# Splitting the second latent head group by token halves, and moving half of the output projection between its second halves

## The chip, the cores and the metric

The kernel runs on one core of one Trainium2 chip. The metric is the time of one execution in microseconds on the device. The core has five engines that work side by side, each through its own queue in order: TensorE (PE in the profile; its weight loads are PEld), VectorE (DVE), ScalarE (ACT), GpSimd (POOL) and SyncE (SP), which issues all DMA transfers of this kernel. "x512" and the like are the elements per partition of an instruction; there are 128 partitions.

## What is computed

One layer of a streaming encoder: 1024 tokens of width 1024, two groups of attention heads side by side, one output projection, then a gated MLP with a causal convolution of width 3. Cut to what matters here:

```python
q = rmsnorm(q_lat @ w_q_up);  k, v = split(rmsnorm(kv_lat) @ w_kv_up)      # latent attention, 8 heads
o_mla = softmax(mask(q @ k.T * 96 ** -0.5)) @ v                            # chunk-causal, 1024 x 1024
o_ca  = chunk_attention(cq, ck, cv, rel_bias)                              # 8 heads, band of 9 chunks
mixed = concat([o_mla, o_ca]) @ w_out
x = x + g_a * mixed                                                        # gated residual
h = rmsnorm(x) * (1 + sc_m) + sh_m                                         # "modulated values"
u = causal_dwconv(h @ w_up);  gate, val = split(u)
x = x + g_m * ((silu(gate) * val) @ w_down)
```

The mask lets token block i (128 tokens) see blocks 0 to i, so the first 512 tokens need only the keys of the first 512.

## The kernel before, in words

Matrix products with float32 accuracy are made of three matmuls each: every operand is split into a high part (a rounded copy, `hi_of`, line 71 or 75) and a low part (the rest, `lo_of`, line 82), and high x high, high x low and low x high are summed in PSUM (`gemm3`, lines 150 to 152). A pair of such parts for 512 columns is called a page.

A scheduler orders the instructions of each engine when the program is built. It goes by the order in which the kernel writes them, by priorities (`tc.high_priority` around scores and values), and by which buffers a pool has. Tiles with the same tag share the buffers of that tag; the next tile waits until the oldest buffer is free.

Attention runs through units: a unit is one head and one half of the tokens (`g` 0 or 1, four query blocks each). First come 16 units of the band heads, then the latent heads in two groups of four (`gr` 0 and 1), each head's first half followed by its second half (the list `units`). Per query block, `scores` makes the scores on TensorE, takes the maximum on VectorE, the exponential on ScalarE, scales to a high half on POOL (line 71, `hl`, three buffers) and a low half on VectorE (line 700), and has SP transpose both by DMA (line 702, `PT`, three buffers; blocks wider than 640 in two pieces). `values`, three blocks later, multiplies by the value rows on TensorE (line 713); after four blocks the two parts of the output are joined (lines 720 and 721) and stored to `oT_d` (line 722). A second half has seven pieces to transpose, a first half four.

Between these steps `pace` lets a list of fillers issue their matmuls, in proportion to the unit's own cost (`R_CA` 1.9, `R_MLA` 0.5): the projections of the inputs, and last `f_oca`, which multiplies the band heads' output by its half of `w_out` and stores the partial sums to `part_d`. Side work (`f_ada`) makes the modulation rows.

After attention, for each of eight token tiles t (from line 868): the latent output `ol` is loaded and split, multiplied by the other half of `w_out` (`op`, 24 matmuls), added to the loaded partial `pa` (line 884), multiplied by the gate row `gabc` (885), added to the residual `x1` (886), stored (887), squared and summed (888), and scaled by the inverse root mean square (891). After tile 3, eight pages of modulated values of the first 512 tokens are transposed and scaled (`mod_T`, lines 855 to 857, two PSUM buffers); they give the pages `b11` and `b21`.

The MLP's up projection is a scheme of seven block products over token halves (as in Strassen's method). It needs the pages b11, b21 (first half), b22 (second half) and t1 to t4 (sums and differences). After tile 7 a loop over k = 0 to 3 makes, for each k, the transposes of the second half and then one page each of t3, t1, b22, t2, t4 (lines 942 to 952). Then `ff_tile` runs for 22 tiles of the hidden width; tile 0's first product needs t3 and the split of the weight difference `ws3` ("ws", line 1012; "wc", its split). The down projection ends the kernel.

## Time and profile before

| | us |
|---|---|
| three timed runs, median (lowest, highest) | 1463.82 (1462.19, 1465.44) |
| profiled execution, span from first to last instruction | 1461.0 |
| PE busy in it | 1273.7 (87%) |
| DVE busy | 1028.2 (70%) |
| POOL busy | 780.0 (53%) |
| ACT busy | 611.7 (42%) |

Of the profiled execution its span is what is shown. A page of the profile gives busy times, the span in 40 slices, the groups of instructions by line, and the DMA issues. The trace behind it can be asked for busy times in chosen stretches, for the instructions in order of time, and for what ended an engine's idle time. A row of the timeline has the start, the length, the engine, the line, the operation, what it writes and reads, how many are merged, and in brackets the idle time before it with its releaser. A row of groups has the count after "x", then busy time, the mean length of one in ns, and the idle time before. Line numbers are those of the kernel before, where nothing else is said.

### The profile page before, as it was taken

Reading aid. Unit: us, or ns where it says so; the run is one execution under the profiler, and the core shown is the slowest. Engines: PE = TensorE matmul, PEld = TensorE weight load, DVE = VectorE, ACT = ScalarE, POOL = GpSimd, SP = SyncE. Lnnn points to the kernel's source line nnn. Section 1 sums busy time; section 2 is a strip of 40 time slices with the busy share of each in tenths; the row PEclk is TensorE's granted clock in tenths of the full one; section 3 lists DMA queues with packets and bytes.
Section 4 is the critical chain, followed back from the end, with each engine's and each line's share of the span. In section 5 each row is a group of like instructions: output and inputs, shape, how many; then the busy total and the mean of one; then the engine's idle time right before and its main releaser. Section 6 shows DMA issues by size and latency. Waiting matters only on the chain.

```text
span 1461.0 us, 20153 instructions
## 1 busy us (share of the span) xinstructions
PE 1273.7 (87%) x6836; PEld 1053.1 (72%) x6836; DVE 1028.2 (70%) x1830; ACT 611.7 (42%) x1190; POOL 780.0 (53%) x717
## 2 busy tenths in 40 slices
PE   3859989998867788885776999999999998999997
PEld 2749878886746666764555888788888887887885
DVE  6874776476798968772487887777777777566653
ACT  4544354343455545443273434334444433332331
POOL 5263554274555745444545555566555555665662
PEclk9979987999788899996887999999999999999998
DMA  7323547455522577869611323322222234446442
GB/s 282 134 71 75 131 113 150 126 122 116 115 64 45 127 153 161 175 139 270 223 72 63 111 100 108 109 87 87 87 87 87 77 137 162 151 144 237 148 142 101
DMA packets 218595, 185.94 MB, mean 127 GB/s; under 512 B 148086, under 2 KB 183034, under 8 KB 217468
## 3 DMA queue, kind: packets, MB, share of 16 engines
q1 hardware_dynamic: 218492, 184.66, 44.0%
q8 instruction: 54, 0.88, 0.2%
q14 instruction: 49, 0.40, 0.1%
HBM read 121.17 MB, written 28.84 MB: 103 GB/s over the span
## 4 chain that ended last, share of the span: by engine, by line
PE 39%; DMA 18%; DVE 16%; POOL 12%; issue 11%; ACT 3%; SPq 1%; DVEq 0%; POOLq 0%; ACTq 0%
POOL wds L82 5%; PE p L921 4%; PE p L923 4%; PE p L922 4%; DMA aw<-w_ada 4%; DMA PTm<-hlm 3%; DMA wu<-w_up 3%; PE sc L655 3%; PE dnp L1064 2%; PE dnp L1066 2%; PE dnp L1065 2%; PE sm L655 2%; DMA PTc<-hlc 2%; DVE adacc L243 2%; DMA cl<-oT_d 1%
## 5 line engine op out<-in xcount | busy, mean ns | idle before, releaser
L82 POOL TENSOR_TENSOR wds<-wd,wds 128x512 fp32r<-128x512 f32 x88 | 153.6, 1766 | 100.7 <-ACT wds L75 100.7
L82 POOL TENSOR_TENSOR wc<-ws,wc 128x512 fp32r<-128x512 f32 x22 | 65.4, 2975 | 134.7 <-ACT wc L75 134.7
L1054 DVE TENSOR_TENSOR wd<-wd,gmbc 128x1024 f32<-128x1024 f32 x44 | 69.4, 1577 | 80.7 <-DMA wd<-w_down 78.1
L1064 PE MATMUL dnp<-wds,g 128*128 128x512 f32 x308 | 119.9, 391 | 2.8 <-DVE xo L1072 2.3
L1066 PE MATMUL dnp<-wds,g 128*128 128x512 f32 x308 | 118.5, 390 | 3.8 <-DVE g L82 3.8
L75 ACT ACTIVATE wds<-wd 128x512 fp32r<-128x512 f32 x88 | 54.8, 624 | 157.8 <-PE dnp L1066 152.7
L1065 PE MATMUL dnp<-wds,g 128*128 128x512 f32 x308 | 119.6, 389 | 0.0
L71 POOL TENSOR_SCALAR hlm<-Pm,rim 128x512 f16<-128x512 f32 (+4 forms) x88 | 66.5, 760 | 58.1 <-DMA PTm<-hlm 37.0
L71 POOL TENSOR_SCALAR hlc<-Pc,ric 128x640 f16<-128x640 f32 (+2 forms) x64 | 45.6, 715 | 79.2 <-DVE ric L683 40.1
L700 DVE SCALAR_TENSOR_TENSOR hlm<-Pm,rim,hlm 128x512 f16<-128x512 f32 (+4 forms) x88 | 66.1, 758 | 23.3 <-POOL hlm L71 23.0
L1012 DVE TENSOR_TENSOR ws<-wu,wu 128x512 f32<-128x512 f32 x22 | 28.1, 1279 | 75.6 <-DMA wu<-w_up 75.6
L655 PE MATMUL sm<-mk,mq 96*128 96x512 f32 (+3 forms) x288 | 71.1, 378 | 10.3 <-ACT Pm L680 9.3
L82 DVE TENSOR_TENSOR g<-gr,g 128x512 fp32r<-128x512 f32 x44 | 71.0, 1616 | 11.4 <-ACT g L75 11.4
L998 DVE SCALAR_TENSOR_TENSOR u<-c,pk,u 128x1023 f32<-128x1023 f32 x44 | 77.4, 1765 | 1.8 <-ACT u L997 1.8
L1033 ACT ACTIVATE u<-u 128x1024 f32<-128x1024 f32 x22 | 23.4, 1063 | 132.0 <-DVE u L999 132.0
L713 PE MATMUL pvm<-PTm,vt 128*128 128x128 f16 x576 | 49.4, 239 | 33.5 <-DMA PTm<-hlm 28.6
L680 ACT ACTIVATE Pc<-sc,mc 128x640 f32<-128x640 f32 (+2 forms) x64 | 42.2, 659 | 86.2 <-DVE mc L670 61.7
L997 ACT ACTIVATE u<-c,pk 128x1024 f32<-128x1024 f32 x44 | 52.3, 1236 | 55.2 <-DVE c L1029 55.2
L430 DVE SCALAR_TENSOR_TENSOR aacc<-aw,cs,aacc 128x256 f32<-128x256 f32 x84 | 44.7, 532 | 43.5 <-DMA aw<-w_ada 42.9
L655 PE MATMUL sc<-k,q 64*128 64x512 f32 (+3 forms) x288 | 70.1, 372 | 5.3 <-ACT Pc L680 3.0
L713 PEld LDWEIGHTS <-vt 128*128 128x128 f16 x576 | 40.6, 108 | 46.3 <-issue 41.2
L1066 PEld LDWEIGHTS dnp<-wds,g 128*128 128x128 f32 x308 | 57.8, 188 | 17.1 <-DVE g L82 5.0
(366 smaller groups left out, 4308.0 us busy)
## 6 DMA issues: line engine op xcount, KB each, us to landing
wu<-w_up SPq DMA_DIRECT2D x44, 512.0 KB, 3.9
wd<-w_down SPq DMA_DIRECT2D x44, 512.0 KB, 4.4
aw<-w_ada SPq DMA_DIRECT2D x96, 128.0 KB, 2.3
g_d<-u SPq DMA_DIRECT2D x22, 512.0 KB, 2.6
gr<-g_d SPq DMA_DIRECT2D x44, 256.0 KB, 3.6
x<-x SPq DMA_DIRECT2D x16, 512.0 KB, 8.0
adaw<-w_ada_a SPq DMA_DIRECT2D x8, 1024.0 KB, 5.6
wq_r<-w_qk SPq DMA_DIRECT2D x32, 128.0 KB, 2.5
```

The lines of the kernel that those rows point to most:

```text
L71: pool.tensor_scalar(o, i, s, 1.0, op0=MUL, op1=MUL)
L82: (pool if eng == "p" else dve).tensor_tensor(o, i, f32(hi), op=SUB)
L655: last = pe.matmul(s[:, c:c + w], qpg[rs_, a, q], kpgs[kh][rs_, b, ko:ko + w], start=(a == 0 and b == 0), stop=(a == 1))
L700: dve.scalar_tensor_tensor(hl[:, w:2 * w], pp, ri[:], hl[:, :w], op0=MUL, op1=SUB)
L713: last = pe.matmul(u.pv[:, c], u.vst(j), mov, start=(x == 0), stop=(x == len(todo) - 1))
L921: pe.matmul(pt, sh, pg[:, 0], start=(k == 0), stop=False)
L922: pe.matmul(pt, sh, pg[:, 1], start=False, stop=False)
L998: dve.scalar_tensor_tensor(u[:, 1:], c[:, :S - 1], pk[:, cv + 1:cv + 2], u[:, 1:], op0=MUL, op1=ADD)
L1054: dve.tensor_tensor(raw[:], raw[:], gmbc[:], op=MUL)
L1064: pe.matmul(pts[t][n], sh, w[n][:, 0], start=(j == 0), stop=False)
L1065: pe.matmul(pts[t][n], sh, w[n][:, 1], start=False, stop=False)
L1066: pe.matmul(pts[t][n], sl, w[n][:, 0], start=False, stop=(j == NF - 1))
```

## The change

The second group's units are put in another order: first the first halves of its four heads, then the four second halves, beginning with head 3. So that keys of the first halves are still there for the second halves, those of three heads are kept in buffers of the tag `v16`, which held values of the band heads. `R_MLA` goes from 0.5 to 0.95, so `f_oca` ends with the first halves. A new filler, `f_first`, then issues what stood behind attention for tokens 0 to 511: the loads of `ol`, `x`, the gate row and the partials, the projection in column halves, residual, norm, and the eight transposed and scaled pages `v0`. These pages use the one PSUM buffer of tag "T". They are copied by DMA to another pool (`v0c`), where the rest of the kernel reads them. The loop behind attention keeps tiles 4 to 7. The pages of the second half are written kind by kind: all transposes, then t3 for the four k, then t2, t1, t4 and b22. The two parts of a unit's output are joined in the output's own buffer.

```diff
-R_CA, R_MLA = 1.9, 0.5
+R_CA, R_MLA = 1.9, 0.95
...
+    def f_first():
+        wo.extend(load_wo(0, n, "a", "p") for n in range(2))
+        ga = []
+        for n in range(2):
+            ga.append(G["v"].tile([P, 512], F32, name=f"gah{n}", tag="Gv", bufs=8))
+            sp.dma_start(ga[n][:], ga_d[:, n * 512:(n + 1) * 512])
+        xs = []
+        for t in range(4):
+            lo = rtile(f"ol{t}", (P, 4, P), F32R)
+            hi = rtile(f"oh{t}", (P, 4, P), F32R)
+            sp.dma_start(f32(lo[:]), oT_d[0:4, :, t * P:(t + 1) * P].rearrange("k p t -> p k t"))
+            hi_of("a", hi[:], f32(lo[:]))
+            lo_of("p", lo[:], f32(lo[:]), hi[:])
+            x1 = pgtile([P, D], F32, f"x1_{t}")
+            sp.dma_start(x1[:], I["x"][t * P:(t + 1) * P, :])
+            for n in range(2):
+                c = slice(n * 512, (n + 1) * 512)
+                pa = qtile(f"pa{t}_{n}")
+                sp.dma_start(pa[:], part_d[t][:, c])
+                pt = ps.tile([P, 512], F32, name=f"op{t}_{n}", tag="mm", bufs=2)
+                yield from gemm3_f(pt[:], [(hi[:, k], lo[:, k], wo[n][k][:, 0], wo[n][k][:, 1]) for k in range(4)])
+                dve.tensor_tensor(pa[:], pa[:], pt[:], op=ADD)
+                pool.tensor_tensor(pa[:], pa[:], ga[n][:], op=MUL)
+                pool.tensor_tensor(x1[:, c], x1[:, c], pa[:], op=ADD)
+                act.activation(pa[:], x1[:, c], AF.Square, accum_out=ss2[:, t, n:n + 1])
+            sp.dma_start(x1_d[t], x1[:])
+            pool.tensor_tensor(ss2[:, t, 0:1], ss2[:, t, 0:1], ss2[:, t, 1:2], op=ADD)
+            rsqrt_mean(r2[:, t:t + 1], ss2[:, t, 0:1], D)
+            act.activation(x1[:], x1[:], AF.Copy, scale=r2[:, t:t + 1])
+            xs.append(x1)
+        for k in range(ND):
+            pt = ps.tile([P, 512], F32, name=f"ht_ps2_{k}_0", tag="T", bufs=TB)
+            for j in range(4):
+                pe.transpose(pt[:, j * P:(j + 1) * P], xs[j][:, k * P:(k + 1) * P], ident[:])
+            v0[k] = g3([P, 512], F32, f"v0_{k}")
+            act.activation(v0[k][:], pt[:], AF.Identity, scale=modT[:, 2, k:k + 1], bias=modT[:, 3, k:k + 1])
+            yield 436
...
+        if tag == "v16":
+            hi, lo = [apg.tile([P, 512], F32R, name=f"{name}_{i}", tag="v16", bufs=6)[:] for i in "hl"]
...
-                    act.activation(sb[r0], u.pv[r1], AF.Copy, scale=inv[r1])
-                    dve.scalar_tensor_tensor(dst[r0], u.pv[r0], inv[r0], sb[r0], op0=MUL, op1=ADD)
+                    act.activation(dst[r0], u.pv[r1], AF.Copy, scale=inv[r1])
+                    dve.scalar_tensor_tensor(dst[r0], u.pv[r0], inv[r0], dst[r0], op0=MUL, op1=ADD)
...
+            kept = gr == 1 and g == 0 and hh < 3
...
-               ("m", f_m()), ("up0", f_up(0)), ("up1", f_up(1)), ("oca", f_oca())]
+               ("m", f_m()), ("up0", f_up(0)), ("up1", f_up(1)), ("oca", f_oca()), ("first", f_first())]
+    half_done = [False]
...
+            if key == "first" and not half_done[0]:
+                return None
...
-    units += [mla_unit(gr, hh, g) for gr in range(2) for hh in range(4) for g in range(2)]
+    units += [mla_unit(0, hh, g) for hh in range(4) for g in range(2)]
+    units += [mla_unit(1, hh, 0) for hh in range(4)]
+    first_half = 4 * len(units)
+    units += [mla_unit(1, hh, 1) for hh in (3, 0, 1, 2)]
...
-            pace(u.values(i), R_CA if u.band else R_MLA)
-    need(["oca"])
-    for _ in side[0]:
-        pass
-    wo = [load_wo(0, n, "a", "v" if n else "p") for n in range(2)]
+            cost = u.values(i)
+            if n - DEPTH + 1 == first_half:
+                need(["oca"])
+                for _ in side[0]:
+                    pass
+                half_done[0] = True
+            pace(cost, R_CA if u.band else R_MLA)
+    need(["first"])
...
+    for k in range(ND):
+        v = vtile(f"v0c_{k}")
+        sp.dma_start(v[:], v0[k][:])
+        v0[k] = v
...
-    for t in range(NT):
+    for t in range(4, NT):
...
-        lo_of("p", lo[:], f32(lo[:]), hi[:])
-        x1 = tb.tile([P, D], F32, name=f"x1_{t}", tag="x1", bufs=8)
+        lo_of("v" if t % 2 else "p", lo[:], f32(lo[:]), hi[:])
+        x1 = tb.tile([P, D], F32, name=f"x1_{t}", tag="x1", bufs=4)
...
-        if t % 4 == 3:
-            h = t // 4
-            if h == 0:
-                for k in range(ND):
-                    v0[k] = mod_T(k, 0)
-                    bpage("b11" if k < 4 else "b21", k % 4, v0[k], "v" if k % 2 else "p")
+    for k in range(ND):
+        bpage("b11" if k < 4 else "b21", k % 4, v0[k], "v" if k % 2 else "p")
...
+    b12 = [mod_T(k) for k in range(4)]
+    b22 = [mod_T(k) for k in range(4, ND)]
     for k in range(4):
-        b12, b22 = mod_T(k, 1), mod_T(k + 4, 1)
-        t3 = tb.tile([P, 512], F32, name=f"t3_{k}", tag="v", bufs=11)
-        dve.tensor_tensor(t3[:], b22[:], b12[:], op=SUB)
+        t3 = vtile(f"t3_{k}")
+        dve.tensor_tensor(t3[:], b22[k][:], b12[k][:], op=SUB)
         bpage("t3", k, t3, "v")
-        dve.tensor_tensor(b12[:], b12[:], v0[k][:], op=SUB)
-        bpage("t1", k, b12, "v")
-        bpage("b22", k, b22, "v")
-        dve.tensor_tensor(b22[:], b22[:], b12[:], op=SUB)
-        bpage("t2", k, b22, "v")
-        dve.tensor_tensor(v0[k + 4][:], v0[k + 4][:], b22[:], op=SUB)
+    for k in range(4):
+        dve.tensor_tensor(b12[k][:], b12[k][:], v0[k][:], op=SUB)
+        t2 = vtile(f"t2_{k}")
+        dve.tensor_tensor(t2[:], b22[k][:], b12[k][:], op=SUB)
+        bpage("t2", k, t2, "v")
+        dve.tensor_tensor(v0[k + 4][:], v0[k + 4][:], t2[:], op=SUB)
+    for k in range(4):
+        bpage("t1", k, b12[k], "v")
+    for k in range(4):
         bpage("t4", k, v0[k + 4], "v")
+    for k in range(4):
+        bpage("b22", k, b22[k], "v")
```

More of the change, by code (lines that the diff above doesn't have):

```diff
@@ L615, in qk_page @@
             pe.transpose(pt[:rows, j * P:(j + 1) * P], src(j), ident[:])
-        pg = at.tile([P, 2, 512], F32R, name=name, tag=tag, bufs=bufs)
+        if tag == "v16":
+            hi, lo = [apg.tile([P, 512], F32R, name=f"{name}_{i}", tag="v16", bufs=6)[:] for i in "hl"]
+        else:
+            pg = at.tile([P, 2, 512], F32R, name=name, tag=tag, bufs=bufs)
+            hi, lo = pg[:, 0], pg[:, 1]
         if gain is None:
-            act.activation(pg[:rows, 0], pt[:rows], AF.Copy)
-            dve.tensor_tensor(pg[:rows, 1], pt[:rows], f32(pg[:rows, 0]), op=SUB)
-        else:
-            act.activation(pg[:rows, 0], pt[:rows], AF.Copy, scale=gain)
-            dve.scalar_tensor_tensor(pg[:rows, 1], pt[:rows], gain, f32(pg[:rows, 0]), op0=MUL, op1=SUB)
-        return pg
+            act.activation(hi[:rows], pt[:rows], AF.Copy)
+            dve.tensor_tensor(lo[:rows], pt[:rows], f32(hi[:rows]), op=SUB)
+        else:
+            act.activation(hi[:rows], pt[:rows], AF.Copy, scale=gain)
+            dve.scalar_tensor_tensor(lo[:rows], pt[:rows], gain, f32(hi[:rows]), op0=MUL, op1=SUB)
+        return hi, lo
     class Unit:
@@ L654, in scores @@
                         for b in range(2 - a):
-                            last = pe.matmul(s[:, c:c + w], qpg[rs_, a, q], kpgs[kh][rs_, b, ko:ko + w],
+                            last = pe.matmul(s[:, c:c + w], qpg[a][rs_, q], kpgs[kh][b][rs_, ko:ko + w],
                                              start=(a == 0 and b == 0), stop=(a == 1))
@@ L765, in mla_unit @@
         u.prep = prep
[L766 removed]
+        u.need = ["up1"] if gr or g else ["up0"]
         u.needv = []
@@ L784, in fill_step @@
                 continue
-            if key not in ("v0", "up0", "up1", "oca"):
+            if key not in ("v0", "up0", "up1", "oca", "first"):
                 nside[0] += c
@@ L864, in bpage @@
         B[nm, k] = pg
-    ss2 = cst.tile([P, NT], F32, name="ss2")
-    r2 = cst.tile([P, NT], F32, name="r2")
     xn2 = {}
```

32 lines of the change are left out of this document (18 added, 14 removed).

## The prediction

> **What bounds it now.** I read the page first, then busy times stage by stage, then the chain of waits from 640 to 800 us, then the order in which the changed program's instructions stand on each queue.
>
> ```profile
> span 1461.0 us, 20153 instructions
> PE   3859989998867788885776999999999998999997
> PEclk9979987999788899996887999999999999999998
> ```
>
> The span is 1461.0 us; the three timed runs have a median of 1463.8, 2.8 more, and I add my difference to that median. TensorE is full from the 22nd slice (767 us on) and has holes before it. The stages, with PE busy time first:
>
> ```profile
> core 0: us, PE busy (x) PEld busy (x) DVE busy (x) ACT busy (x) POOL busy (x), PEclk, DMA share, GB/s
> 500.00:571.60 71.60, 62.61 (x409) 49.24 (x408) 53.51 (x134) 33.63 (x73) 35.65 (x41) 0.92 0.73 158
> 571.60:649.00 77.40, 64.28 (x447) 51.90 (x447) 58.61 (x145) 38.77 (x82) 36.50 (x44) 0.93 0.75 158
> 649.00:676.00 27.00, 15.97 (x123) 13.42 (x120) 13.83 (x30) 8.60 (x19) 10.52 (x13) 0.73 0.82 168
> 676.00:742.70 66.70, 51.26 (x209) 40.30 (x210) 28.44 (x25) 22.06 (x38) 40.09 (x34) 0.83 0.70 249
> 742.70:777.80 35.10, 14.32 (x73) 10.55 (x71) 30.99 (x46) 24.44 (x40) 5.20 (x7) 0.71 0.04 15
> 795.10:1180.00 384.90, 381.22 (x1672) 313.17 (x1671) 302.79 (x277) 160.25 (x225) 227.50 (x140) 1.00 0.26 95
> ```
>
> From 795 us TensorE is busy 381 of 385 us at full clock: 1672 matmuls, 0.230 us each. Nothing after that point is edited, so the change is worth what it moves the first product of the MLP (the "wc" product of tile 0). Before that stand latent attention (to 676), the output projection of eight token tiles (to 742.7), and the pages (to 777.8), where VectorE is busy 31 of 35 us and TensorE 14. The marks I count from:
>
> ```profile
> 669.64 0.69 POOL L71 TENSOR_SCALAR hlm<-Pm,rim 128x512 f16<-128x512 f32 x1 [1.44 <-DMA PTm<-hlm]
> 674.95 1.01 PE L713 MATMUL pvm<-PTm,vt 128*128 128x128 f16 x8 [1.71 <-DMA PTm<-hlm]
> 742.32 0.39 PE L152 MATMUL op<-wo,ol 128*128 128x512 f32 x1
> 751.26 1.13 DVE L891 TENSOR_SCALAR x<-x,r 128x1024 f32<-128x1024 f32 x1 [2.15 <-DMA x_d<-x]
> 754.29 0.69 DVE L944 TENSOR_TENSOR t<-hv,hv 128x512 f32<-128x512 f32 x1 [1.30 <-ACT hv L857]
> 776.38 0.68 DVE L1012 TENSOR_TENSOR ws<-wu,wu 128x512 f32<-128x512 f32 x1
> 777.84 0.80 PE L921 MATMUL p<-t,wc 128*128 128x512 f32 x1 [14.11 <-ACT wc L75]
> ```
>
> The last attention value ends at 675.96 and the MLP begins at 777.84: 101.9 us. The last POOL half of a probability piece starts 6.3 us before that value ends. The 36 VectorE page instructions run from 754.29 to 776.38, and the subtraction that feeds the first product stands behind them all on VectorE.
>
> **Attention, part one of the sum.** The change puts 96 projection matmuls (tokens 0 to 511) among the four second halves; 84 of them stand before the last value, the last 12 behind it. Does attention have room? I cut the stage at the first transpose of each half unit and counted the old filler (tile oc), short halves first, long ones after:
>
> ```profile
> 596.00:606.20 10.20, 0.38 (x2) 0.30 (x2) 0.00 (x0) 0.00 (x0) 0.83 0.59 129
> 544.90:557.60 12.70, 7.04 (x25) 4.01 (x23) 0.00 (x0) 0.60 (x1) 1.00 0.64 115
> 557.60:571.60 14.00, 2.06 (x7) 1.06 (x6) 0.00 (x0) 1.18 (x2) 1.00 0.97 211
> 606.20:621.90 15.70, 9.19 (x36) 6.00 (x34) 0.00 (x0) 1.16 (x2) 1.00 0.94 203
> 523.30:544.90 21.60, 12.13 (x37) 7.68 (x36) 0.00 (x0) 1.79 (x3) 0.84 0.71 158
> ```
>
> 23 more matmuls lengthen a short half by 2.5 us (0.11 each); 29 or 30 more lengthen a long one by 1.7 or 7.6 (0.06 or 0.25). I take 0.10: 84 x 0.10 = 8.4 us. The ends are nothing, if all of it runs in the holes (PE is busy 143 of the 176 us, so 33 are idle), and 84 x 0.230 = 19.3 us, if TensorE pays for each. The other load of the new filler falls on POOL:
>
> ```profile
> L71 POOL TENSOR_SCALAR hlm<-Pm,rim 128x512 f16<-128x512 f32 (+4 forms) x70 | 48.4, 695 | 52.9 <-DMA PTm<-hlm 36.3 <-DVE rim L683 6.3 <-DVE sm L673 3.9
> L82 POOL TENSOR_TENSOR cl<-cl,ch 128x512 fp32r<-128x512 f32 x16 | 21.9, 1368 | 28.6 <-ACT ch L75 26.3 <-PE mq_ps L615 2.2
> ```
>
> In the last long half seven pieces of 0.7 us (4.9) get eight 512-wide operations of about 1.3 us and three short ones (some 1.5) between them: 16.8 us on a queue that has 14 to 16. I add 0.6 us for that, so the last value comes 9 us later (675.96 to 685). Multiplications by the gate row that were VectorE's are POOL's here; each also waits for its load of the stored partial, for which there are two buffers, and the pieces queued behind it wait too. That is the same POOL time, counted once. Weight loads and splits (16 instructions) are those of before, earlier.
>
> **From the last value to the MLP, part two.** Prices:
>
> ```profile
> L857 ACT ACTIVATE hv<-ht_ps,modT 128x512 f32<-128x512 f32 x16 | 11.8, 775 | 7.0 <-PE ht_ps L855 7.0
> L888 ACT ACTIVATE pa<-x 128x1024 f32<-128x1024 f32 x8 | 8.5, 1059 | 16.5 <-POOL x L886 13.7 <-DVE x L886 2.7
> L884 DVE TENSOR_TENSOR pa<-pa,op 128x1024 f32<-128x1024 f32 x8 | 9.7, 1219 | 24.5 <-PE op L152 24.5
> L116 POOL TENSOR_TENSOR r<-ss,nhalf 128x1 f32<-128x1 f32 x8 | 6.4, 799 | 0.5
> 743.00 1.03 PE L855 MATMUL ht_ps<-ident,x 128*128 128x128 f32 x8
> 752.80 1.45 ACT L857 ACTIVATE hv<-ht_ps,modT 128x512 f32<-128x512 f32 x2 [2.08 <-PE ht_ps L855]
> 760.95 1.12 PE L855 MATMUL ht_ps<-ident,x 128*128 128x128 f32 x4 [1.54 <-ACT hv L857]
> 681.65 0.80 PE L150 MATMUL op<-wo,oh 128*128 128x512 f32 x1 [5.69 <-ACT oh L75]
> ```
>
> (a) Token tile 3 has to be finished: 17.3 us. Its second partial can be loaded only when the square of tile 2 has freed a buffer. From the last POOL piece: five 1.3 us operations, three short ones, two waits for the first partial of tile 3 give 13.2 us until that square is done; then, with the gaps, load 3.8 (behind a 512 KB store), add 0.8, multiply and add on POOL 2.6, square 0.8, mean and power 1.2, scale 1.2: 23.6, less the 6.3 us up to the last value. The floor is 10, if the partials wait for nothing. (b) Eight pages of transposes through one PSUM buffer, each followed by its activation: 1.12 + 0.78 + 0.1 = 2.0 us, 16 us in all; warm (the eight transposes in 1.03 us at 743.00) it would be 12. Before, these pages lay under the projection of tiles 4 to 7.
>
> The Trainium skill, page "TensorE: Matmul & The Clock Gate", section "Part 4: PE-mode transpose", says that transposes do not count as the activity that raises the clock. By that the 16 us hold; if transposes did raise it the sum would be 4 us less. The quoted row is cold but had idle time before it, so the trace does not decide it.
>
> (c) In the SP order the eight copies of those pages (line 909 of the changed kernel) stand ahead of the four x loads, the gate row and the first load of the second half's attention output. SP waits in order, so that output is asked for only after the eighth page, behind five transfers of 512 KB:
>
> ```profile
> wu<-w_up SPq DMA_DIRECT2D x44, 512.0 KB, 3.9
> ol<-oT_d SPq DMA_DIRECT2D x8, 256.0 KB, 4.0
> DMA packets 5757, 9.76 MB, mean 349 GB/s; under 512 B 400, under 2 KB 3472, under 8 KB 5755
> ```
>
> The second row is on the page, the third is 676 to 704 us, where the queue was full. A lone output load issued 2.8 us after the page would land at 6.8; 2.9 MB at 349 to 410 GB/s behind 3 us of issue and latency land at 10.2. I take 10.2 and 0.7 for its high part: 10.9 (7.5 to 12). Before, nothing stood ahead of those loads but weights, and the projection began at 681.65. (d) Four token tiles are 96 matmuls, 22.1 us, and 2 us for a cold start as at 681.65: 24.1. The gain of the change is here: before, eight tiles took 742.71 - 681.65 = 61 us with their waits. (e) Tile 7 from its last matmul to its scaled rows took 752.39 - 742.71 = 9.7 us; I take 8.7, since POOL has no page work beside VectorE. (f) Scaled rows to the first product took 25.5 us. **Pages kind by kind** do not shorten it: the same 36 VectorE instructions stand ahead of the "ws" subtraction in the changed order too. They begin later: VectorE's first needs the fifth activation (5.9 us after the scaling by cold transposes and 0.68 us a page), where it needed the second (1.9). I add 3.7: 29.2.
>
> Sum: 17.3 + 16 + 10.9 + 24.1 + 8.7 + 29.2 = 106.2 us against 101.9, 4.3 more.
>
> **The rest** I put at nothing: three kept key heads in old value buffers and half outputs combined in place remove no instruction and wait for stores 10 us old; the product of the first two page kinds with tile 0 (24 matmuls, 5.5 us) lies under (e), and stood there in part before; the lower halves of odd tiles go from POOL to VectorE under running matmuls.
>
> **Sum.** 9 + 4.3 = 13.3 us: the span 1474.3, the time 1463.8 + 13.3 = **1477.1 us**.
>
> **Rivals.** First, faster: attention gets shorter. A short half takes 10.2 us and more for four transposes (2.5 us each), a long one 14 for seven (2.0). If the short ones are slow only because they alternate with long ones, four in a row at 2.0 save 12 us (11 less 8, four times), and the filler runs free in waits. Then the last value comes 12 us earlier, and 4.3 - 12 gives -7.7: 1456.1. It decides at a last value before 671.7. For it speak the idle PE; against it that a short tile has the same chain (maximum, exponential, two halves, transpose) as a long one. Second, the filler is paid in full: TensorE and POOL queues hold each other up, 19.3 + 4.3 = 23.6: 1487.4. Third, the pages do work kind by kind: VectorE's 19th of 36 instructions ends the first kind, so the MLP could begin 17 x 0.61 = 10.4 us earlier: 1466.7; the order of VectorE speaks against it, since "ws" stands last. Fourth, the tail's waits are at their floors (10, 12 and 7.5 in (a) to (c)): 14.7 less, 1462.4.
>
> **Chances.** Forecast 0.53 (own range 1468 to 1484), attention shorter 0.11, paid in full 0.20, kind by kind 0.04, floors 0.12. A measurement of this kernel can tell about 0.2%, 2.9 us. Faster by more: the first rival and a little of the fourth, 0.13; within: most of the fourth and part of the third, 0.12; slower 0.75. The range leaves out most of the first rival and the top of the second: 1460 to 1490.
>
> **What would show it.** The last value (pvm, then om) at about 685 and not before 672; after it TensorE nearly idle for 40 us but for 32 transposes with an activation after each four; copies v0c on SP, then x, then ol; the wc product behind all 36 page instructions, 106 us after the last value; equal times from there on. I am wrong if attention ends early, if ol is issued before the copies end, or if wc runs while pages are still made. Weakest is the price of a filler matmul, 0 to 0.23 us, and the two-buffer chain of (a).

## The result, and the profile after

The changed kernel takes 1482.88 us (median of four runs, 1481.71 to 1487.18) against 1464.57 for the kernel before (four runs, 1462.19 to 1465.44): a ratio of 1.0127, with a 95% interval of 1.0103 to 1.0151. It is slower, as forecast, by 18.3 us where 13.3 were forecast. The profiled execution has a span 20.4 us longer. From its page:

```profile
span 1481.4 us, 20209 instructions
PE   3859989998968788986384999999999999999996
PEclk9879987999789898988596999999999999999999
```

A slice is 37.0 us. Before the long row of nines stand a 3 (704 to 741 us, most of the stretch between the last attention value and the projection of tile 4), an 8 (that projection) and a 4 (the pages of the second half). The stages after, cut at the marks the prediction used (PE busy first):

```profile
572.20:618.80 46.60, 41.77 (x251) 33.75 (x249) 32.90 (x87) 24.93 (x55) 18.64 (x25) 0.93 0.71 180
618.80:691.70 72.90, 57.39 (x369) 43.53 (x368) 47.74 (x85) 28.56 (x57) 48.45 (x51) 0.86 0.84 192
691.70:709.10 17.40, 3.67 (x15) 2.50 (x14) 2.71 (x4) 6.27 (x10) 9.51 (x13) 0.73 0.32 111
709.10:724.40 15.30, 8.28 (x29) 5.19 (x29) 0.00 (x0) 6.28 (x10) 0.00 (x0) 0.50 0.32 120
724.40:735.70 11.30, 0.00 (x0) 0.00 (x0) 6.30 (x4) 4.74 (x9) 6.29 (x4) 0.50 0.90 332
735.70:760.40 24.70, 24.56 (x97) 19.67 (x98) 13.82 (x10) 6.21 (x10) 11.64 (x11) 0.90 0.50 179
760.40:768.80 8.40, 6.21 (x30) 4.84 (x28) 5.05 (x5) 2.34 (x5) 1.48 (x4) 1.00 0.30 121
768.80:797.40 28.60, 5.49 (x26) 3.74 (x26) 23.20 (x40) 17.84 (x29) 0.00 (x0) 0.61 0.00 0
```

The first two rows are the second latent group: the four first halves, then the four second halves. The other six are the steps (a) to (f) of the prediction: 17.4, 15.3, 11.3, 24.7, 8.4 and 28.6 us, 105.7 in all, where it said 17.3, 16, 10.9, 24.1, 8.7 and 29.2, 106.2 in all. The same group before, from the last value of the first group to its own:

```profile
575.00:676.00 101.00, 76.85 (x542) 62.40 (x540) 69.89 (x167) 44.53 (x93) 44.91 (x54) 0.88 0.76 161
```

So the second latent group went from 101.0 to 119.5 us, 18.5 more, on 78 more matmuls and 22 us more of POOL. Of those matmuls 65 are filler: the group holds 75 of the old filler (tile oc) and 84 of the new one, where it held 94 of the old. The whole account of the 20.4 us: the first group ends 2.8 earlier (572.2 instead of 575.0), the second takes 18.5 more, the tail 3.8 more (105.7 against 101.9), tile 0 of the MLP 1.0 less, everything from tile 1 on 1.8 more (20.3, to within rounding). The table gives the same marks for every kernel run; M is the end of the first group, L the last value, O the first projection matmul of tile 4, W the first product of tile 0, N the first matmul of tile 1, all in us and from the timelines. The two stages on both sides of O are left empty where the projection of tiles 0 to 3 lies between L and O.

| kernel | M to L | L to O | O to W | M to W | W to N | N to end | time us |
|---|---|---|---|---|---|---|---|
| before | 101.0 | | | 202.8 | 17.3 | 665.9 | 1464.6 |
| changed | 119.5 | 44.0 | 61.7 | 225.2 | 16.3 | 667.7 | 1482.9 |
| e1 filler let go late | 124.6 | 34.7 | 63.0 | 222.4 | 16.4 | 668.8 | 1481.8 |
| e2 a third of the matmuls | 111.4 | 45.8 | 61.9 | 219.1 | 16.7 | 668.6 | 1481.1 |
| e3 gate on VectorE | 119.7 | 32.4 | 61.7 | 213.9 | 16.8 | 668.3 | 1471.8 |
| e4 four partial buffers | 125.6 | 21.5 | 61.6 | 208.6 | 16.3 | 667.5 | 1469.6 |
| e5 order only (from before) | 100.3 | | | 205.9 | 17.1 | 664.6 | 1471.6 |
| e6 two PSUM buffers | 117.7 | 37.0 | 62.1 | 216.8 | 17.3 | 665.8 | 1475.4 |
| e7 load of tile 4 ahead | 118.3 | 33.7 | 69.5 | 221.5 | 16.9 | 669.3 | 1483.4 |
| e8 weight parts ahead | 116.4 | 44.4 | 43.2 | 204.0 | 27.0 | 673.0 | 1478.5 |
| e9 four repairs | 129.8 | 19.5 | 62.2 | 211.4 | 17.2 | 668.7 | 1479.1 |
| e10 e9 and weight parts | 130.4 | 19.5 | 43.0 | 193.0 | 27.0 | 672.8 | 1473.8 |
| e11 pages only (from before) | 101.8 | | | 189.0 | 30.5 | 668.6 | 1470.1 |
| e12 e9 and loads ahead | 126.5 | 7.8 | 70.7 | 205.0 | 17.1 | 667.2 | 1473.6 |

Times of e1 to e8 are single runs, the others are medians; the ratios given with an interval are worked out over all runs and differ a little from those of the medians. Runs of the kernel before made beside the experiments lie between 1461 and 1474, so a single time is good to about 6 us; stages are read from them instead. Between the changed kernel, e6, e7 and e8, which do not differ up to L, M to L varies from 116.4 to 119.5: about 3 us is the scatter of a stage.

### The profile page after: what moved, and what is told of

Same layout as the page of the kernel before. It is cut to its first block, busy times and chain, and to the rows that moved or that the text cites. A ratio compares the mean times of both kernels' runs of the same rounds, so it can differ in the third digit from the quotient of the medians.

```text
span 1481.4 us, 20209 instructions
## 1 busy us (share of the span) xinstructions
PE 1285.4 (87%) x6836; PEld 1059.8 (72%) x6836; DVE 1030.9 (70%) x1826; ACT 618.6 (42%) x1202; POOL 790.6 (53%) x733
## 4 chain that ended last, share of the span: by engine, by line
PE 53%; DMA 14%; DVE 11%; POOL 9%; issue 8%; ACT 3%; SPq 1%; DVEq 0%; POOLq 0%; ACTq 0%
PE p L980 8%; PE p L982 8%; PE p L981 8%; POOL wds L82 5%; PE sc L701 3%; DMA PTm<-hlm 3%; DMA aw<-w_ada 3%; PE dnp L1129 2%; PE dnp L1130 2%; PE dnp L1131 2%; DVE adacc L243 2%; PE pvc L759 1%; PE sm L701 1%; PE ipv L150 1%; PE ipv L151 1%
## 5 line engine op out<-in xcount | busy, mean ns | idle before, releaser
L1130 PE MATMUL dnp<-wds,g 128*128 128x512 f32 x308 | 119.5, 389 | 0.0
L71 POOL TENSOR_SCALAR hlm<-Pm,rim 128x512 f16<-128x512 f32 (+4 forms) x88 | 65.3, 748 | 44.9 <-DMA PTm<-hlm 30.5
L71 POOL TENSOR_SCALAR hlc<-Pc,ric 128x640 f16<-128x640 f32 (+2 forms) x64 | 45.8, 717 | 74.1 <-DVE ric L729 37.2
L746 DVE SCALAR_TENSOR_TENSOR hlm<-Pm,rim,hlm 128x512 f16<-128x512 f32 (+4 forms) x88 | 70.2, 808 | 21.4 <-POOL hlm L71 21.4
L1131 PEld LDWEIGHTS dnp<-wds,g 128*128 128x128 f32 x308 | 57.8, 188 | 17.1 <-DVE g L82 5.1
L1129 PEld LDWEIGHTS dnp<-wds,g 128*128 128x128 f32 x308 | 57.8, 188 | 15.1 <-DVE xo L1137 2.7
L1130 PEld LDWEIGHTS dnp<-wds,g 128*128 128x128 f32 x308 | 57.8, 188 | 11.8
```

The lines of the kernel that those rows point to most:

```text
L71: pool.tensor_scalar(o, i, s, 1.0, op0=MUL, op1=MUL)
L746: dve.scalar_tensor_tensor(hl[:, w:2 * w], pp, ri[:], hl[:, :w], op0=MUL, op1=SUB)
L1129: pe.matmul(pts[t][n], sh, w[n][:, 0], start=(j == 0), stop=False)
L1130: pe.matmul(pts[t][n], sh, w[n][:, 1], start=False, stop=False)
L1131: pe.matmul(pts[t][n], sl, w[n][:, 0], start=False, stop=(j == NF - 1))
```

## The experiments

The prediction's tail came out term by term; its attention term did not (9 forecast, 15.8 later by the last value, 18.5 by the group's length). Theory A: TensorE pays for each filler matmul (the second rival, 0.19 to 0.23 us each). Theory B: the order of the units costs it. Theory C: the filler's other work, its POOL operations and its two-buffer chain of loads, holds up the queues, which run in order.

### e1_behind: the filler let go after the last value

```diff
-                half_done[0] = True
...
+    half_done[0] = True
     need(["first"])
```

> The changed kernel, but the filler with the first half's projection is let go only after the last attention value, so that the four second halves run with no filler at all; everything else is as changed. This measures the price of the 84 matmuls in attention. In the changed kernel the last value ends at 691.7 us of the span. Theory A (TensorE pays for each matmul, and the order of the units costs nothing): 84 x 0.19 to 0.23 less, the last value at 672 to 676. Theory B (the new order of the units itself is slower): it stays above 684. The whole is then longer than the changed kernel, since the same matmuls with their two-buffer chain stand bare behind attention: 1482.9 - 17 + 8 x 3.5 = about 1494 us.

Missed, and not what the edit was for. The scheduler orders instructions by readiness, not by where they are written: 96 projection matmuls still ran before the last value, nearly all in the last two second halves (2 in that of head 0, 70 in that of head 1, 24 in that of head 2), and the last value came at 697.1. It prices nothing; it shows only that the filler does not run later for being let go later in the program's text. M to W is 2.8 us less than in the changed kernel, within scatter.

### e2_third: two thirds of the filler's matmuls left out

```diff
-                yield from gemm3_f(pt[:], [(hi[:, k], lo[:, k], wo[n][k][:, 0], wo[n][k][:, 1]) for k in range(4)])
+                for k in range(4):
+                    with tc.issue_after(trail[-1 - LAG]):
+                        pe.matmul(pt[:], hi[:, k], wo[n][k][:, 0], start=k == 0, stop=k == 3)
+                    if k % 2:
+                        yield 6 * (512 / 2.4 + 2.5)
```

> The changed kernel with only the high x high matmul of the first half's projection (4 of 12 for each column half; the two correction products are left out, so the result lacks them); all loads, splits, gate products, squares and the pacing stay. Theory A (TensorE time is what the filler costs): 56 of the 84 matmuls in attention fall away at 0.19, so the last value comes 10.6 us earlier, at 681, and the time is about 1471. Theory C (what costs is the chain of load, add, gate product, residual, square, through two buffers and the POOL queue, with TensorE waiting in order): less than 3 us, last value at 689 or later, time 1480.

Between the two. Twenty-four filler matmuls are left before the last value instead of 84, and the group is 8.1 us shorter (119.5 to 111.4): 0.135 us per matmul. But it is still 10 us longer than before with nearly the same number of matmuls. Its four first halves and its four second halves:

```profile
575.00:620.10 45.10, 40.09 (x250) 32.11 (x249) 33.08 (x88) 25.06 (x56) 18.17 (x24) 0.96 0.73 187
620.10:686.40 66.30, 46.28 (x309) 35.42 (x308) 44.59 (x84) 27.13 (x53) 46.43 (x46) 0.77 0.88 202
```

POOL is busy 64.6 us in the group, where it had 44.9 before, so the filler's other work is the first suspect for the 10 us. The next run says where they stand.

### e5_order_only: the new order of the units alone

```diff
-    units += [mla_unit(gr, hh, g) for gr in range(2) for hh in range(4) for g in range(2)]
+    units += [mla_unit(0, hh, g) for hh in range(4) for g in range(2)]
+    units += [mla_unit(1, hh, 0) for hh in range(4)]
+    units += [mla_unit(1, hh, 1) for hh in (3, 0, 1, 2)]
```

(on the kernel before, with the kept keys and the joined halves of the change)

> The kernel before with the new order of the units alone (second latent group: four first halves, then the second halves of heads 3, 0, 1, 2, keys kept, output parts joined in place); the old filler at its old ratio, the whole projection behind attention as before. Theory B (the order itself costs what attention got longer by): last value 685 to 692 us of the span instead of 676. Theory C (the order is free, the new filler's chain costs): 673 to 679 and the time within 3 us of the kernel before. My first rival before the result (first halves in a row are faster): 664.

The group takes 100.3 us (101.0 before): the order is free at the old filler's ratio, and theory B falls. The last value is at 682.5 only because this execution reached the group 7 us later (M at 582.2); the expectation was written in marks of the span, which carry that. The first halves in a row are faster (34.1 us for four, from the ends of their last values, against 42.2 when they alternated), and the second halves slower by nearly as much (66.2 against 58.8), so the first rival of the prediction saw something real that came back within the group. The same two stretches as for e2:

```profile
582.20:616.30 34.10, 30.13 (x191) 24.07 (x192) 27.17 (x77) 20.27 (x46) 16.25 (x22) 0.89 0.72 157
616.30:682.50 66.20, 51.72 (x360) 42.60 (x359) 42.18 (x90) 25.04 (x48) 27.99 (x32) 0.81 0.84 162
```

Beside e2 they move the suspicion. The 11.1 us between the two runs lie in the first halves (45.1 against 34.1), where the new filler has not been let go: none of its POOL operations stands there, and POOL is busy 18.2 and 16.3 us. The second halves, where all of the new filler's POOL work is, take 66.3 and 66.2 us. What fills the first halves is the old filler, which at an `R_MLA` of 0.95 ends there:

| | first halves, us | old filler matmuls in them | second halves, us | filler matmuls in them |
|---|---|---|---|---|
| before | 42.2 | 40 | 58.8 | 54, old |
| e5 order only | 34.1 | 35 | 66.2 | 59, old |
| e2 a third of the matmuls | 45.1 | 75 | 66.3 | 24, new |
| changed | 46.5 | 75 | 72.9 | 84, new |

In a row the first halves leave TensorE little room: it is busy 30.1 of 34.1 us in e5 and 41.7 of 46.5 in the changed kernel. Of these 11.5 us more, 10.95 are the old filler's matmuls (22.87 against 11.92 us busy); the 12 score matmuls that run ahead into the stretch (63 against 51) take 1.8, less what overlaps. So theory A fits the first halves, for matmuls that the prediction left out. In the second halves the 60 matmuls between the changed kernel and e2 are worth 6.6 us. What the new filler's other work costs there can only be estimated: e2 has 35 filler matmuls fewer than e5 and gains nothing, which at 0.135 us each would be 5 us. No run changes `R_MLA` alone; this division is read from the stages of single executions, with their 3 us of scatter.

### e3_gate_dve and e4_pa4: POOL's share, and the buffers

```diff
-                pool.tensor_tensor(pa[:], pa[:], ga[n][:], op=MUL)
-                pool.tensor_tensor(x1[:, c], x1[:, c], pa[:], op=ADD)
+                dve.tensor_tensor(pa[:], pa[:], ga[n][:], op=MUL)
+                dve.tensor_tensor(x1[:, c], x1[:, c], pa[:], op=ADD)
```

> The changed kernel with the gate product and the residual sum of the filler on VectorE instead of POOL. Theory A: no change of the last value (691.7 within 2 us). Theory C, POOL part (probability pieces wait behind 1.3 us operations on POOL): the last value 4 to 8 us earlier, at 684 to 688, and the time 1475 to 1479.

```diff
+        pap = [pgtile([P, D], F32, f"pap{i}") for i in range(2)]
...
-                pa = qtile(f"pa{t}_{n}")
-                sp.dma_start(pa[:], part_d[t][:, c])
+                pa = pap[t % 2][:, c]
+                sp.dma_start(pa, part_d[t][:, c])
```

> The changed kernel with four half-row buffers for the loaded partials instead of two (two idle page buffers taken). Theory A: last value unchanged (691.7 within 2 us). Theory C, buffer part (the load waits for the square of two pieces earlier and stands on the transfer queue behind transposes that wait for POOL): last value 5 to 7 us earlier, and the finish of token tile 3, 17.4 us from the last value to its scaled rows, falls to 10 to 13; the time is then 1470 to 1474.

First the chain as it stands in the changed kernel, from its timeline in the last second half:

```profile
676.83 0.53 SPq L633 DMA_DIRECT2D pa<-part_d  x1
681.05 0.69 DVE L636 TENSOR_TENSOR pa<-pa,op 128x512 f32<-128x512 f32 x1 [2.62 <-DMA pa<-part_d]
681.79 0.79 PE L150 MATMUL op<-wo,oh 128*128 128x512 f32 x1 [4.17 <-DVE pa L636]
681.81 1.72 POOL L637 TENSOR_TENSOR pa<-pa,gah 128x512 f32<-128x512 f32 x1 [2.31 <-DMA ol<-oT_d]
684.09 0.63 PE L152 MATMUL op<-wo,ol 128*128 128x512 f32 x1
684.75 0.69 POOL L71 TENSOR_SCALAR hlm<-Pm,rim 128x512 f16<-128x512 f32 x1
```

The partial is asked for at 676.83, lands four microseconds later, and only then can VectorE add it and free a PSUM buffer. TensorE stood 4.17 us with the next filler matmul at the head of its queue, attention values behind it, and came back on a slow clock (rows of 0.63 us instead of 0.40, a matmul every 0.43 us instead of 0.23). POOL stood 2.31 us at the gate product (its row names a transfer, but the addition that it needs ended at 681.74), and the last probability piece, behind it, was scaled at 684.75. The waits of TensorE on that addition, from the last first half to past tile 3, in the changed kernel and in e3 (engine, waiting line, released by; us in total, times, longest):

```profile
PE op L150 <- DVE pa L636: 6.3, 2, 4.2
```

```profile
PE op L150 <- DVE pa L636: 0.5, 1, 0.5
```

In e4 the line is gone. Both edits miss where they were aimed and gain elsewhere. The group did not get shorter (119.7 and 125.6 us): the filler, no longer held, put all of its 96 matmuls and 3 and 10 of the page transposes ahead of the last value. But tile 3 was ready 5.3 us after the last value in e3, and 6.4 before it in e4, instead of 17.4 after, and O came 11.4 and 16.4 us earlier counted from M. So the chain is a true cost of the change, some 11 to 16 us up to O, and it was spread over attention and step (a).

### e6_ht_mm: two PSUM buffers for the pages

```diff
-            pt = ps.tile([P, 512], F32, name=f"ht_ps2_{k}_0", tag="T", bufs=TB)
+            pt = ps.tile([P, 512], F32, name=f"ht_ps2_{k}_0", tag="mm", bufs=2)
```

> The changed kernel with the eight transposed pages of the first half going through the two PSUM buffers of the projection instead of one. In the changed kernel they take 15.2 us from the scaled rows of tile 3 to the last activation (2.0 a page). If one buffer is the cause, a page then takes the slower of four transposes (0.9 to 1.1 us) and one activation (0.8), 9 to 10 us in all, and the copies, the loads behind them and everything later come 5 to 6 us earlier: 1477. If the transposes themselves are the limit, less than 2 us.

Here the theory holds: the pages take 7.9 us instead of 15.3, and the projection of tile 4 begins 7 us sooner after the last value (37.0 against 44.0). The stage and its transposes:

```profile
708.40:716.30 7.90, 6.36 (x26) 4.65 (x26) 0.00 (x0) 5.98 (x9) 0.00 (x0) 0.58 0.54 197
```

```profile
709.75 5.70 PE L648 MATMUL ht_ps<-ident,x 128*128 128x128 f32 x24 [0.66 <-ACT v L650]
```

In the changed kernel each page's transposes took 1.12 of 2.0 us, and the granted clock was 0.50 over the whole 15.3 us. Here twenty-four transposes follow each other for 5.7 us without a hole, and the clock rises at the end of them:

```profile
711.70:715.00 3.30, 3.27 (x15) 2.58 (x15) 0.00 (x0) 2.46 (x4) 0.00 (x0) 0.50 0.71 262
715.10:718.40 3.30, 0.35 (x3) 0.11 (x1) 0.95 (x1) 3.30 (x7) 1.48 (x2) 1.00 0.84 292
```

The Trainium skill's sentence on transposes (page "TensorE: Matmul & The Clock Gate", section "Part 4: PE-mode transpose"), that they do not count as the activity that raises the clock, does not hold here: from 708.40 to 715.1 TensorE ran nothing but transposes, and the granted clock went from 0.50 to 1.00. The second half's pages show the same (in e9 0.50 from 758.60 to 761.90, with 15 transposes and nothing else on TensorE, and 1.00 from 762.10). The measurement decides. Step (b)'s 16 us came out all the same: with one buffer TensorE was busy 8.28 of the 15.3 us, and the clock stayed at 0.50.

### e7_ol4_ahead: the transfer queue

```diff
+    o4 = [tb.tile([P, 4, P], F32R, name=f"o{i}4", tag=f"o{i}4", bufs=1) for i in "lh"]
+    sp.dma_start(f32(o4[0][:]), oT_d[0:4, :, 512:640].rearrange("k p t -> p k t"))
+    hi_of("a", o4[1][:], f32(o4[0][:]))
+    lo_of("p", o4[0][:], f32(o4[0][:]), o4[1][:])
     for k in range(ND):
         v = vtile(f"v0c_{k}")
```

> The changed kernel with the attention output of tile 4 loaded and split from buffers of its own, its load ahead of the eight page copies on the transfer queue. If the queue order is what costs 11.3 us between the last page and the first projection matmul of tile 4, that falls to 1 to 2 us and the time by 8 to 10, to 1473 to 1475; if the later loads (tile 5, the x rows, the partials) are as late as before and hold the projection, less than 4 us of it remain.

The queue before the edit:

```profile
710.49 14.36 SPq L909 DMA_DIRECT2D v0c<-v  x8
724.90 2.03 SPq L940 DMA_DIRECT2D x<-x  x4
726.97 0.54 SPq L932 DMA_DIRECT2D gabc<-ga_d  x1
727.56 0.47 SPq L936 DMA_DIRECT2D ol<-oT_d  x1
735.02 0.63 ACT L75 ACTIVATE oh<-ol 128x512 fp32r<-128x512 f32 x1 [6.51 <-DMA ol<-oT_d]
```

SP issues in order and waits for each page; the load that TensorE needs is issued at 727.56, lands before 735.02. With the load ahead of the copies tile 4 began 0.6 us after the last page, 10 us sooner, as expected. But only the wait moved: tile 5's own load was then late, and TensorE waited for it 4.76 us,

```profile
738.39 0.79 PE L150 MATMUL op<-wo,oh 128*128 128x512 f32 x1 [4.76 <-ACT oh L75]
```

so O to W grew from 61.7 to 69.5, and of the 10 us between L and O 2.4 remain at W; the single time, 1483.4, shows no gain. The second reading of the expectation was the right one.

### e8_ws_tb and e11_before_ws: kind by kind

```diff
+    ws3 = mt("w2", [P, 2, 512], "ws3_0")[:, 0]
+    wc0 = tb.tile([P, 2, 512], F32R, name="wc0", tag="w", bufs=2)
...
+    dve.tensor_tensor(ws3, ra[:, :512], rb[:, :512], op=SUB)
...
     for k in range(4):
         t3 = vtile(f"t3_{k}")
```

(and the same for wd; in e11, on the kernel before, with wc0 alone and the changed order of the pages)

> The changed kernel with the weight differences and splits for the first two products of tile 0's second part (t3 and t2) made ahead of the pages, in buffers that are free then. In the changed kernel all 36 page instructions of VectorE stand ahead of the difference, so that the first product starts at 797.4 us although its last page part was made at 785.8. If that is why kind by kind brought nothing, the first product starts 11 us earlier, the second 8 earlier, and the rest is ready by the end of the pages: 6 to 8 us off the time, 1475 to 1477. If the pages or the splits on POOL are the limit, under 3.

> The kernel before with the pages of the second half written kind by kind and the weight difference and split of the first product made ahead of them; units, attention and projection as before. It tells how much of a gain belongs to the pages and not to the token halves. The first product starts 8 to 12 us earlier than 777.8, the second, whose split still stands behind all pages, 0 to 2 earlier; with what VectorE gives back the time is 0 to 3 us under the kernel before.

In the changed kernel the lower half of the last t3 page is made on VectorE at 785.08, and the difference that the first product also needs stands eleven microseconds later, behind the last page:

```profile
785.08 0.69 DVE L82 TENSOR_TENSOR t<-t,t 128x512 fp32r<-128x512 f32 x1
795.92 0.69 DVE L1077 TENSOR_TENSOR ws<-wu,wu 128x512 f32<-128x512 f32 x1
797.40 0.80 PE L980 MATMUL p<-t,wc 128*128 128x512 f32 x1 [21.82 <-ACT wc L75]
```

With the weight parts ahead the first product of e8 starts at 776.50, 20.9 us earlier (18.5 counted from O), which confirms why the pages brought nothing (more than the 11 expected, since its first matmul needs the first t3 page only). Yet tile 1 begins only 10.2 earlier (7.8 counted from O), because the products that follow still wait for their pages, and 5.3 of that is given back later, about half of it where TensorE waits on VectorE's sums. Counted from O, 2.4 us are left at the end, within scatter. The waits in the 412 us from tile 1 on, in the changed kernel and in e8:

```profile
PE p L980 <- DVE c L1085: 2.3, 5, 0.5
```

```profile
PE p L980 <- DVE c L1099: 5.0, 9, 1.2
```

In e11 the first product starts 9.7 us earlier and tile 1 3.5 later (0.6 earlier counted from M): 1470.06 us against 1466.85 (12 and 18 runs), ratio 1.0011 (0.9994 to 1.0028), no difference, where 0 to 3 us less were expected. The pages kind by kind, even with the weight part that they lacked, are worth nothing to the kernel before.

### e9_repaired, e10_repaired_ws and e12_loads_ahead: the repairs together

```diff
-                pool.tensor_tensor(pa[:], pa[:], ga[n][:], op=MUL)
...
+                dve.tensor_tensor(pa, pa, ga[n][:], op=MUL)
...
-    ss2 = cst.tile([P, NT, 2], F32, name="ss2")
+    ss2 = cst.tile([P, NT, 3], F32, name="ss2")
```

(with the edits of e4 and e6; e10 adds that of e8)

> The changed kernel with four of its own costs taken out together: four half-row buffers for the partials, the gate product on VectorE, the first half's pages through two PSUM buffers, and 32 bytes more in the pool of constants. The 32 bytes test a finding of the comparison: in the changed kernel the matmuls on the pages b11 and b21 follow each other every 233.4 ns instead of 226.7, and only these pages stand at another address modulo 64 bytes than before. If the address is the cause, they go back to 226.7 and a tile of the MLP from 19.25 to 19.05 us, 4 us in all. If the buffer chain and the one PSUM buffer are what the change costs, the projection of tile 4 begins at 711 to 717 us (735.7 in the changed kernel, 722.4 with four buffers alone, 728.1 with two PSUM buffers alone), the first product at 772 to 778, and the time is 1453 to 1459, 0.5 to 0.8% under the kernel before. If these costs lie in one another (TensorE pays for the filler anyway), the projection begins at 720 or later and the time is that of the kernel before or above.

> The kernel of e9_repaired with the weight differences and splits for the first two products of tile 0 made ahead of the pages as well (the edit of e8_ws_tb). There the second tile began 10.2 us earlier but half of it was given back, since VectorE, with the gate row beside it, then sets the pace of tiles 2 to 9 (20.0 us instead of 19.25). So 4 to 6 us under e9_repaired are expected: 1447 to 1455. If VectorE's pages are the limit in full, nothing.

e9: 1479.1 us against 1466.85 (6 and 18 runs), ratio 1.0075 (1.0048 to 1.0102); e10: 1473.78, ratio 1.0045 (1.0027 to 1.0064). Both are better than the change and worse than expected (1453 to 1459 and 1447 to 1455 us). The costs lie in one another: from M to O e4 alone won 16.4 us and e6 8.8, e9 with both and the gate product on VectorE 14.2, and from M to W e9 with 211.4 us is no better than e4 alone with 208.6. Once the chain is loose, TensorE is what the second half of head 1 waits for:

```profile
658.90:689.00 30.10, 26.16 (x141) 20.17 (x140) 22.09 (x37) 13.48 (x26) 22.26 (x26) 0.89 0.73 189
```

63 filler matmuls crowd into this one unit, PE is busy 26.2 of 30.1 us, and the group takes 129.8. Here theory A holds too. Of what is left between L and O, 19.5 us, most is the transfer queue, as the last run shows:

```diff
+    ox = {}
+    for t in range(4, 6):
...
+        ox[t] = lo, hi
+    x1s = {}
+    for t in range(4, NT):
+        x1s[t] = tb.tile([P, D], F32, name=f"x1_{t}", tag="x1", bufs=4)
+        sp.dma_start(x1s[t][:], I["x"][t * P:(t + 1) * P, :])
     for k in range(ND):
         v = vtile(f"v0c_{k}")
...
-    ss2 = cst.tile([P, NT, 2], F32, name="ss2")
+    ss2 = cst.tile([P, NT, 5], F32, name="ss2")
```

(against the changed kernel, with the other edits of e9)

> The kernel of e9_repaired with the loads of attention output for tiles 4 and 5 and of the four x rows ahead of the eight page copies on the transfer queue, in buffers of their own, and with the pool of constants 96 bytes longer than in the changed kernel instead of 32, so that b11 and b21 stand at 96 modulo 128 as in the kernel before. In e9_repaired the projection of tile 4 began 19.5 us after the last value, 8 of it issue of copies and loads, and tile 5 was held by its own load in e7_ol4_ahead. If the queue order is the cause, it begins 8 to 10 us after the last value and the first product comes 9 to 12 us earlier against the last value (81.7 us after it in e9_repaired, now 70 to 73). If the later partials are still late, 3 or less. The address: spacing on b11 and b21 228.9 to 229.7 ns in e9_repaired, 226.7 if the remainder modulo 128 decides. Time 1465 to 1471, that is within 0.3% of the kernel before: the change repaired is then level with it.

L to O falls to 7.8 us as expected. But L to W is 78.5, not 70 to 73, since tile 6 then waits 6.5 us for its own load, which stands behind the copies. The projection's stage in e12, and TensorE's largest waits from L to W:

```profile
710.80:745.60 34.80, 27.27 (x97) 21.01 (x98) 19.35 (x14) 11.12 (x19) 19.28 (x15) 0.83 0.77 275
```

```profile
PE p L994 <- ACT wc L75: 21.8, 1, 21.8
PE op L150 <- ACT oh L75: 12.2, 3, 6.5
```

1473.64 us against 1466.15 (11 and 15 runs), ratio 1.0044 (1.0023 to 1.0065), where 1465 to 1471 were expected. With the buffers, the gate product and the first loads repaired, the change still loses: M to W is 205.0 us where the kernel before has 202.8. e12 keeps `R_MLA` at 0.95 (its first halves take 45.2 us) and lacks the weight parts of e8; a kernel with either changed as well was not run. No version that beats the kernel before was found.

## Why the prediction was right, and where its size was off

- **The tail, (a) to (f).** Right term by term (105.7 for 106.2), with its mechanisms: the two-buffer chain held tile 3 (e3 and e4 take (a) away), one PSUM buffer held the pages (e6), the transfer queue held tile 4 (e7), and the weight difference stood behind all pages (e8). The size of (b) held, though transposes did raise the clock once they filled TensorE (e6). (d) and (e) agree in size; no run tested them.
- **Attention, 8.4 us for 84 matmuls.** This is the term that was mis-sized: the group took 18.5 us more. It priced the new filler in the second halves and left out the old filler that has to make room for it. The old filler's matmuls in the first halves went to 75, from 40 before and 35 in e5, and those halves take 46.5 us where e5 takes 34.1. The 0.10 us per matmul was read from halves that alternate, where TensorE had holes; four first halves in a row have few. For the new matmuls alone the price was not far off: e2 gives 0.135.
- **Attention, "I add 0.6 us for that" (POOL) and "Weight loads and splits (16 instructions) are those of before, earlier" (put at nothing).** Too little, but by how much is open (the estimate above is 5 us in the second halves of e2). The prediction counted POOL's busy time where its waits count. In the changed kernel POOL waited, in the four second halves, at the head of its queue for weight splits and gate products, with probability pieces behind:

```profile
POOL wo L82 <- DVE om L766: 4.2, 1, 4.2
POOL pa L637 <- DVE pa L636: 3.3, 2, 1.8
POOL wo L82 <- ACT wo L75: 3.1, 2, 2.8
```

  The gate product's part is shown by e3 and e4 for tile 3, not for the group, whose length they left. What the weight splits cost was not tried.
- **The first group, put at nothing,** ended 2.8 us earlier with the larger pace of the old filler; that is within the scatter of M (570.7 to 576.6 in the kernels with this code, but for e10).
- **Step (f), 29.2 for 28.6.** The 3.7 us that it adds are 4.0 by its own figures (5.9 less 1.9); it makes no difference here.
- **From the first product on, "equal times".** Off by 0.8 us: tile 0 1.0 less, tile 1 to the end 1.8 more (below).
- **The rivals.** Attention shorter: the first halves did get faster in a row, but the second halves gave it back (e5). Paid in full: its 19.3 us for attention are nearer to the 18.5 measured than the forecast's 9, and its 1487.4 us are 4.5 from the result where 1477.1 is 5.8; but it laid them on the 84 new matmuls in the second halves, where 6.6 us are shown, and the rest stands in first halves that it did not look at. Kind by kind: refuted as I argued, and it stays so with the weight parts ahead (e8, e11). Tail at its floors: no.
- **Luck.** The tail was understood; the attention term was half of what came, and of that only a part for the reason given. That the sum still came within some 5 us is in part luck, the more so as the first group of the profiled execution ended 2.8 us early, within scatter, which hides as much of the term at the last value (15.8 us late, not 18.5).

## What to carry to other kernels

When new filler pushes old filler forward, price the old filler too, at the place where it lands: here 40 more matmuls stood in a stage with TensorE already busy 30 of 34 us. Filler that brings waits with it is priced by what it puts at the head of an in-order queue, not by its busy time alone: count, for each engine and for the transfer queue, what stands behind an instruction that waits. Repairs of costs that lie behind one another don't add up (16 and 9 us made 14), and a wait taken from the first of several loads moves to the second; compare the stage from its beginning to its end, not at the mark that the edit aims at. Work moved ahead of a stage only pays if everything its consumer needs is moved too: here one weight difference kept 36 page instructions in front of a product that needed 8 of their results, and even with it moved the later products waited for their pages (e8, e11).

## What was not expected of the hardware

The matmuls of the MLP on the pages b11 and b21 are slower in the changed kernel, at a granted clock of 1.00 and with the same instructions around them. Durations (min, median, max in ns) of the first product's high x high and high x low matmuls between 900 and 1100 us, in the kernel before, the changed kernel and e12:

```profile
L921 PE MATMUL p<-b,wa x40: 389/389/798, 910.7 to 1089.8; 128*128 128x512 f32 x40
L922 PE MATMUL p<-b,wa x40: 389/389/395, 911.0 to 1090.0; 128*128 128x512 f32 x40
```

```profile
L980 PE MATMUL p<-b,wa x40: 393/396/792, 910.1 to 1090.5; 128*128 128x512 f32 x40
L981 PE MATMUL p<-b,wa x40: 390/394/397, 910.4 to 1090.8; 128*128 128x512 f32 x40
```

```profile
L994 PE MATMUL p<-b,wa x40: 390/394/794, 914.5 to 1094.0; 128*128 128x512 f32 x40
L995 PE MATMUL p<-b,wa x40: 387/392/398, 914.7 to 1094.3; 128*128 128x512 f32 x40
```

From start to start they follow about every 227 ns before and every 233 in the changed kernel, those on the other pages every 227 in both, but for the first two t3 pages; over 21 tiles of 24 such matmuls 6 ns make about 3 us, an estimate. The program places the pages from byte 25056 of a partition on before and in e11 (227 ns), 25088 in the changed kernel (233), 25120 in e9 (230), 25184 in e12 (233). The last is 96 modulo 128 like the first, so the remainder modulo 64 or 128, which e9 and e12 were to test, does not decide it. Nor does a page's own address alone: the first two t3 pages stand at bytes 147424 and 151520 in the changed kernel and in e11 alike, and their matmuls follow every 224 to 241 ns in the one and every 227 in the other. What does is open.
